# Up projections: four products of high weights, then four of low weights, for each tile of x

## The chip, the cores and the metric

The kernel runs on one core of a Trainium2 chip (trn2). The metric is device time in microseconds for one execution of the whole program. The engines that matter are TensorE (PE for its products, PEld for the loads of the weights that stand still in its array), VectorE (DVE), ScalarE (ACT) and SyncE (SP), whose queue issues the DMA loads. TensorE's products add up in eight banks of PSUM, each 512 fp32 columns wide.

## What is computed

A two-layer encoder trunk on 256 tokens of width 2048: each layer is a token mixer (layer 0 dilated and grouped-query attention, layer 1 latent attention) and a gated convolutional channel mixer. All is fp32. Cut to the part that the change touches:

```python
def conv_glu(h, w_up, conv_w, conv_b, w_down):
    u = h @ w_up                                   # (256, 2048) @ (2048, 11264)
    gate, val = u[..., :D_FF], u[..., D_FF:]       # D_FF = 5632
    gate = depthwise_conv3(gate, conv_w, conv_b)
    return (jax.nn.gelu(gate, approximate=False) * val) @ w_down

# in each layer:
h = rms_norm(x, p['ffn_pre'])
x = x + rms_norm(conv_glu(h, *p['ffn']), p['ffn_post'])
```

## The kernel before

Every fp32 product is made from parts that TensorE takes at a faster rate (the type fp32r): an operand is split into a high part, its rounding to fp32r, and a low part, the rest. A product is then high x high + high x low + low x high; low x low is dropped.

**Weights.** They come in chunks of 128 x 1024, in a fixed order over the whole program. `weights()` returns the current chunk's two parts and issues the work for the next ones: the load by SP's queue into one of four `raw` buffers (line 156), the rounding on ACT into one of three `whi` buffers (line 173), and the subtraction on DVE into one of three `wlo` buffers (line 174). As a rule the parts of two further chunks are issued ahead, so a buffer is written again as soon as the products that read it are done.

**Up projection.** `ffn` runs over 11 groups of 512 gate columns; for each it calls `proj_t` twice, for the gate columns (`pg`, banks of the tag "acc") and for the value columns (`pv`, banks "at"). So there are 22 such calls in a layer and 44 in all. A call has 8 chunks, each with the weights of two tiles of x (k = 2c and 2c + 1; x has 16 tiles of 128 features) for 512 output columns, which are four blocks of 128, one bank each. The weights stand still in the array. What streams through it is x(k): 256 columns of its high part and 256 of its low part side by side. A product with high weights (line 244) streams all 512, giving high x high in one half of the bank and high x low in the other. A product with low weights (line 245) streams the first 256 alone and adds low x high into the first half.

**After a call.** `joined` (lines 305 and 306) copies one half of a bank out on ACT and adds the other on DVE. The gate goes on through the norm's factor (986), the convolution (987 to 990) and gelu (992), the value through 997 and 998 and a split (585, 586). All this shares ACT's and DVE's queues with the splitting of the weights for the next call, which uses the other four banks.

**Around the up projections.** Before the first group, the residual is added (454), x is transposed tile by tile on TensorE (478) and split into `xhl` by ACT and DVE (590, 591); this goes on while the first group's products run. After the last group, `down` runs the down projection (1101, 1102, 1104), partly by a scheme with seven products for eight, whose sums (1005, 76) are made by DVE at its start.

**Order.** The program is written as one list, and a compile-time planner turns it into one queue per engine. It weighs priorities (the order of the program) against its own estimate of when each operand is ready, so instructions of one engine can stand in another order than written. Each queue then runs in order. Transposes and a few others are kept in the written order by `keep_in_program_order`.

Of the kernel before, what the change touches and what calls it, by code (L numbers as in the profile page):

```python
# [16 lines left out]
P = 128  # L17
T = 256
# [68 lines left out]
class Model:  # L87
# [146 lines left out]
    def proj_t(self, nk, x, tag):  # L234

        mm = self.nc.tensor.matmul
        out = [self.psum(tag) for _ in range(4)]
        for c in range(nk // 2):
            hi, lo = self.weights()
            for i in range(4):  # L240
                for kk in range(2):
                    k = 2 * c + kk
                    s = slice(kk * 512 + i * P, kk * 512 + (i + 1) * P)
                    mm(out[i], hi[:, s], x(k), start=k == 0, stop=False)  # L244
                    mm(out[i][:, :T], lo[:, s], x(k)[:, :T], start=False, stop=k == nk - 1)  # L245
            self.tick()
        return out

# [998 lines left out]
```

## Time and profile before

| what | value |
|---|---|
| time, median of 3 runs | 2061.9 us (2061.72 to 2062.07) |
| profiled execution, span from the first to the last instruction | 2060.1 us |
| TensorE products: busy, count | 2043.4 us (99%), 10905 |
| DVE busy | 1478.4 us (72%) |
| ACT busy | 1129.3 us (55%) |
| mean granted TensorE clock | 0.998 |
| products of line 244 (512 columns) | 2816 |
| products of line 245 (256 columns) | 2816 |
| up projections, start of the first to start of the last product | layer 0 from 331.1 us, layer 1 to 1817.9 us |

The profiled execution has no time listed apart from its span; the span is 1.8 us below the median of the runs. In the rows, "idle" is the time an engine stood still in front of an instruction, and what follows the arrow is what ended that idle time. A product's recorded duration runs into the next one's, since products are pipelined; the step from one product's start to the next one's is what it costs in a stream.

### The profile page before, as it was taken

The page shows a single profiled execution, that of the slowest core. Times are in us where ns is not written, and L with a number is a line of the kernel's source. Part 1 is how long each engine was busy: PE and PEld are TensorE (multiplying, and loading weights), DVE is VectorE, ACT ScalarE, POOL GpSimd, SP SyncE. Part 2 cuts the span into 40 slices and gives each one's busy share as a digit, 9 for nine tenths or more (in the row PEclk, how much of TensorE's full clock was granted, in tenths as well). Part 3 has the DMA queues.
Part 4 walks back from the last instruction along what each step waited for, and adds up shares of the span by engine and source line. Part 5 has one row for each costly group of instructions (what it writes and reads, how often), then busy time and mean ns, then how long its engine had stood idle before and what let it go on. Part 6 is the DMA issues. An engine that isn't in the chain of part 4 may idle for free.

```text
span 2060.1 us, 29196 instructions
## 1 busy us (share of the span) xinstructions
PE 2043.4 (99%) x10905; PEld 1750.0 (85%) x10905; DVE 1478.4 (72%) x2263; ACT 1129.3 (55%) x1753; POOL 0.2 (0%) x4
## 2 busy tenths in 40 slices
PE   9999999999999999999999999999999999999998
PEld 7888888888888888888878998888888888888886
DVE  6877757766766767878787875676766766787877
ACT  6655546555555555555465664555555555554553
POOL 0000000000000000000000000000000000000000
PEclk9999999999999999999999999999999999999999
DMA  8545566666566666566655445566566566556664
GB/s 318 176 153 161 166 197 193 186 194 193 185 194 191 185 194 189 184 211 197 203 179 170 124 134 173 176 210 189 185 193 193 184 195 193 185 184 205 204 206 141
DMA packets 108717, 385.96 MB, mean 187 GB/s; under 512 B 12064, under 2 KB 12576, under 8 KB 108576
## 3 DMA queue, kind: packets, MB, share of 16 engines
q1 hardware_dynamic: 108288, 383.83, 59.3%
q8 instruction: 85, 1.39, 0.3%
q14 instruction: 56, 0.46, 0.1%
q10 hardware_dynamic: 288, 0.28, 0.0%
HBM read 381.96 MB, written 2.10 MB: 186 GB/s over the span
## 4 chain that ended last, share of the span: by engine, by line
PE 96%; DVE 3%; issue 0%; ACT 0%; DMA 0%; DVEq 0%; SPq 0%; ACTq 0%
PE ps L244 31%; PE ps L245 16%; PE ps L230 8%; PE ps L231 8%; PE ps L232 8%; PE ps L1104 7%; PE ps L1101 7%; PE ps L1102 7%; PE ps L537 1%; PE ps L300 1%; DVE x L454 1%; DVE wlo L174 1%; PE ps L478 0%; DVE sums L1005 0%; DMA raw<-in_w_in 0%
## 5 line engine op out<-in xcount | busy, mean ns | idle before, releaser
L174 DVE TENSOR_TENSOR wlo<-raw,whi 128x1024 fp32r<-128x1024 f32 (+1 forms) x662 | 807.6, 1221 | 490.3 <-ACT whi L173 487.6
L173 ACT CAST whi<-raw 128x1024 fp32r<-128x1024 f32 (+1 forms) x662 | 694.3, 1050 | 642.7 <-PE ps L244 302.4
L244 PE MATMUL ps<-xhl,whi 128*128 128x512 f32 x2816 | 978.7, 394 | 1.0 <-DVE xhl L591 1.0
L245 PE MATMUL ps<-xhl,wlo 128*128 128x256 f32 x2816 | 779.2, 277 | 0.0
L244 PEld LDWEIGHTS ps<-xhl,whi 128*128 128x128 f32 x2816 | 527.6, 188 | 123.1 <-DVE xhl L591 2.0
L245 PEld LDWEIGHTS ps<-xhl,wlo 128*128 128x128 f32 x2816 | 528.9, 188 | 1.0 <-DVE wlo L174 0.5
L1101 PE MATMUL ps<-whi,gh 128*128 128x512 f32 x584 | 227.3, 389 | 0.0
L1102 PE MATMUL ps<-whi,gl 128*128 128x512 f32 x584 | 227.2, 389 | 0.0
L1104 PE MATMUL ps<-wlo,gh 128*128 128x512 f32 x584 | 182.0, 390 | 0.8 <-DVE wlo L174 0.8
L230 PE MATMUL ps<-whi,xhl 128*128 128x512 f32 x352 | 138.7, 395 | 0.9 <-ACT whi L173 0.8
L231 PE MATMUL ps<-wlo,xhl 128*128 128x512 f32 x352 | 137.6, 391 | 0.0
L232 PE MATMUL ps<-whi,xhl 128*128 128x512 f32 x352 | 137.2, 390 | 0.0
L1104 PEld LDWEIGHTS ps<-wlo,gh 128*128 128x128 f32 x584 | 109.1, 188 | 25.2 <-DVE wlo L174 2.7
L1101 PEld LDWEIGHTS ps<-whi,gh 128*128 128x128 f32 x584 | 109.6, 188 | 22.8
L1102 PEld LDWEIGHTS ps<-whi,gl 128*128 128x128 f32 x584 | 109.6, 188 | 22.8
L230 PE MATMUL ps<-whi,oh 128*128 128x512 f32 x256 | 100.0, 390 | 0.0
L231 PE MATMUL ps<-wlo,oh 128*128 128x512 f32 x256 | 99.7, 389 | 0.0
L232 PE MATMUL ps<-whi,ol 128*128 128x512 f32 x256 | 99.6, 389 | 0.0
L305 ACT COPY half<-ps 128x256 f32<-128x256 f32 x176 | 65.1, 370 | 43.9 <-PE ps L244 34.6
L230 PEld LDWEIGHTS ps<-whi,xhl 128*128 128x128 f32 x352 | 66.0, 188 | 14.5 <-ACT whi L173 1.1
L232 PEld LDWEIGHTS ps<-whi,xhl 128*128 128x128 f32 x352 | 66.1, 188 | 13.9
L231 PEld LDWEIGHTS ps<-wlo,xhl 128*128 128x128 f32 x352 | 66.3, 188 | 13.4 <-DVE wlo L174 0.9
(211 smaller groups left out, 2061.0 us busy)
## 6 DMA issues: line engine op xcount, KB each, us to landing
raw<-in_w_up SPq DMA_DIRECT2D x352, 512.0 KB, 4.1
raw<-in_w_down SPq DMA_DIRECT2D x128, 512.0 KB, 3.9
raw<-in_w_in SPq DMA_DIRECT2D x88, 512.0 KB, 3.7
raw<-in_w_out SPq DMA_DIRECT2D x64, 512.0 KB, 4.1
seven_a<-in_w_down SPq DMA_DIRECT2D x24, 512.0 KB, 4.5
seven_b<-in_w_down SPq DMA_DIRECT2D x24, 512.0 KB, 4.2
gb<-in_post SPq DMA_DIRECT2D x16, 256.0 KB, 3.8
raw<-in_w_qn SPq DMA_DIRECT2D x8, 512.0 KB, 3.6
```

Of the source, the lines that this page charges most:

```text
L173: self.nc.scalar.copy(hi[:, s], raw[:, s])
L174: self.nc.vector.tensor_tensor(out=lo[:, s], in0=raw[:, s], in1=hi[:, s].bitcast(F32), op=ALU.subtract)
L230: mm(ps, lh, rh, start=start, stop=False)
L231: mm(ps, lh, rl, start=False, stop=False)
L232: mm(ps, ll, rh, start=False, stop=stop)
L244: mm(out[i], hi[:, s], x(k), start=k == 0, stop=False)
L245: mm(out[i][:, :T], lo[:, s], x(k)[:, :T], start=False, stop=k == nk - 1)
L300: self.tc.keep_in_program_order(self.nc.tensor.transpose(out, x, self.ident))
L305: self.nc.scalar.copy(b, ps[:, T:])
L1101: mm(bank, xh, w[0][:, c], start=start, stop=False)
L1102: mm(bank, xl, w[0][:, c], start=False, stop=False)
L1104: mm(bank, xh, w[1][:, c], start=False, stop=stop)
```

## The change

In `proj_t`, the loop over the two tiles of x in a chunk becomes the outer one. For each tile, four products of high weights go to the four banks, then four products of low weights go to the same four banks. Each bank gets the same products in the same order of k; the first product of a bank still clears it, and its last product is still the low one of the last tile.

```diff
         for c in range(nk // 2):
             hi, lo = self.weights()
-            for i in range(4):
-                for kk in range(2):
-                    k = 2 * c + kk
-                    s = slice(kk * 512 + i * P, kk * 512 + (i + 1) * P)
-                    mm(out[i], hi[:, s], x(k), start=k == 0, stop=False)
-                    mm(out[i][:, :T], lo[:, s], x(k)[:, :T], start=False, stop=k == nk - 1)
+            for kk in range(2):
+                k = 2 * c + kk
+                s = [slice(kk * 512 + i * P, kk * 512 + (i + 1) * P) for i in range(4)]
+                for i in range(4):
+                    mm(out[i], hi[:, s[i]], x(k), start=k == 0, stop=False)
+                for i in range(4):
+                    mm(out[i][:, :T], lo[:, s[i]], x(k)[:, :T], start=False, stop=k == nk - 1)
             self.tick()
```

## The prediction

> **What bounds the kernel now.** I read the page first: its engines, its chain, its groups.
>
> ```profile
> span 2060.1 us, 29196 instructions
> PE 2043.4 (99%) x10905; PEld 1750.0 (85%) x10905; DVE 1478.4 (72%) x2263; ACT 1129.3 (55%) x1753; POOL 0.2 (0%) x4
> PE 96%; DVE 3%; issue 0%; ACT 0%; DMA 0%; DVEq 0%; SPq 0%; ACTq 0%
> L244 PE MATMUL ps<-xhl,whi 128*128 128x512 f32 x2816 | 978.7, 394 | 1.0 <-DVE xhl L591 1.0
> L245 PE MATMUL ps<-xhl,wlo 128*128 128x256 f32 x2816 | 779.2, 277 | 0.0
> ```
>
> TensorE (PE) is busy for 99% of the span and is 96% of the chain that ended last. L244 and L245 are the 2816 long products (512 columns, high weights) and 2816 short ones (256 columns, low weights) that the change reorders; TensorE idled 1.0 us in front of them in the whole run. Their mean durations (394 and 277 ns) overlap, since matmuls are pipelined, so they are no prices. What counts is start to start. So I went to the table by windows, for a stretch that holds one group of eight chunks, and to the timeline of TensorE, where the first and last row of a run and the count between them give the interval.
>
> ```profile
> 401.21:423.40 22.19, 22.19 (x131) 19.41 (x130) 15.45 (x25) 13.10 (x20) 0.00 (x0) 1.00 0.62 191
> ```
>
> ```profile
> 559.63 0.40 PE L244 MATMUL ps<-xhl,whi 128*128 128x512 f32 x1
> 559.87 0.28 PE L245 MATMUL ps<-xhl,wlo 128*128 128x256 f32 x1
> 559.98 0.39 PE L244 MATMUL ps<-xhl,whi 128*128 128x512 f32 x1
> ...
> 565.87 0.40 PE L244 MATMUL ps<-xhl,whi 128*128 128x512 f32 x1
> ```
>
> The first window's columns are length, then busy time of PE, PEld, DVE, ACT, POOL, then the granted clock (1.00). A group of 64 pairs takes 22.19 us, and TensorE is busy for all of it: 346.7 ns a pair. The timeline agrees: 18 pairs between 559.63 and 565.87, 6.24 us, 346.7 ns a pair. All 2816 pairs are then 976 us, 47% of the span. Nothing but TensorE's own rate sets this time, so the first question is what that rate becomes in the new order.
>
> **The change part by part: the products.** No product is added or removed: each chunk keeps 8 long and 8 short ones, with as many weight loads. Only the neighbours change. Eight products were long, short, long, short, ...; now they are four long, then four short. Of the eight intervals, one long-to-short and one short-to-long stay (together 346.7 ns); three long-to-short and three short-to-long become three long-to-long and three short-to-short. Both new kinds stand elsewhere in this trace: long after long in the output projection (first fence), short after short in layer 1's attention (second).
>
> ```profile
> 259.68 0.39 PE L230 MATMUL ps<-whi,oh 128*128 128x512 f32 x1
> 259.90 0.39 PE L231 MATMUL ps<-wlo,oh 128*128 128x512 f32 x1
> ...
> 303.88 0.39 PE L230 MATMUL ps<-whi,oh 128*128 128x512 f32 x1
> ```
>
> ```profile
> 1142.27 0.28 PE L232 MATMUL ps<-ckv,wlo 128*128 128x256 f32 x1
> 1142.39 0.28 PE L230 MATMUL ps<-cq,whi 128*128 128x256 f32 x1
> ...
> 1145.15 0.28 PE L232 MATMUL ps<-cq,wlo 128*128 128x256 f32 x1
> 1145.27 0.28 PE L230 MATMUL ps<-pT,v 128*128 128x256 f32 x1
> ```
>
> Long to long: 195 intervals in 44.20 us, 226.67 ns. Short to short: 24 intervals from 1142.39 to 1145.27, 2.88 us, 120.0 ns. Together 346.67 ns, what a long-short pair takes now. Two points on a line also give what is paid per product whatever its length: 2 x 120.0 - 226.67 = 13.3 ns, and the pair in alternation pays it twice, no more. So the three swapped pairs cost 3 x (346.67 - 346.7) = 0 in each of the 704 sets of eight (2816 / 4). Bounds: rows are rounded to 0.01 us, so the short interval is known to about 0.4 ns, the long one to 0.05 ns and the pair by the window to 0.2 ns; I allow 0.5 ns, over 2112 swapped pairs +-1.1 us. I take 0.
>
> In the new order every product goes to another bank than the one before it, where now four in a row accumulate into one. The short run above crosses from one psum tile to the next at 1142.27 to 1142.39 and at 1145.15 to 1145.27, and both steps are 0.12 us like the rest; I price the rotation at nothing, inside the same bound.
>
> **The first group of a layer.** There x is still being made when the projection starts.
>
> ```profile
> PE ps L244 <- DVE xhl L591: 1.0, 2, 0.5
> PE ps L1104 <- DVE wlo L174: 0.8, 2, 0.4
> ```
>
> ```profile
> 331.07 0.49 PE L244 MATMUL ps<-xhl,whi 128*128 128x512 f32 x1
> ...
> 331.75 0.28 PE L245 MATMUL ps<-xhl,wlo 128*128 128x256 f32 x1
> 332.51 0.50 PE L244 MATMUL ps<-xhl,whi 128*128 128x512 f32 x1 [0.48 <-DVE xhl L591]
> ```
>
> ```profile
> 331.59 0.87 DVE L591 SCALAR_TENSOR_TENSOR xhl<-ps,gains,xhl 128x256 fp32r<-128x256 f32 x2
> ```
>
> The chain of waits has two waits of 0.5 us on xhl, one per layer. The old order wants the second tile of x after one pair of the first bank; the new one finishes all four banks with the first tile, 4 x 0.347 = 1.39 us of work, first. The two L591 end at 332.46, and the projection's first product started at 331.07, so work for the first tile lasts till 332.46 and the wait goes. I take the whole 0.5 us twice: -1.0 us. Bounds: 0 (the planner orders these products otherwise) and -1.5 us (the 0.76 us step from 331.75 to 332.51 less a normal 0.12 is 0.64 us, and a little more around it, twice). What is late next is the low half of the second chunk's weights, which the new order wants 3 x 0.227 = 0.68 us later than the old.
>
> **Buffers and queues.** The high weights of a chunk are read for the last time four short products before a chunk's end instead of one, 3 x 0.120 = 0.36 us earlier, so the cast that waits for that buffer on ACT, the subtraction on DVE behind it, and the load on SP's queue that waits for the raw buffer come 0.36 us earlier in steady state. None of them is on the path (TensorE idles 0.0 us for weights there), so this is worth nothing, and its cover is the 22.19 us of a group in which DVE works 15.45 and ACT 13.10. The queues' contents stay the same; the planner that orders them may shift some.
>
> The other end is worse off. A bank's sum is finished later: bank 0's last product was the 4th of the last chunk's 16 and becomes the 13th. It used to be done 2 x 0.347 = 0.69 us into the chunk and is now done at 4 x 0.347 + 4 x 0.227 + 0.12 = 2.41 us: 1.72 us later. Bank 1 is 1.15 us later, bank 2 0.57, bank 3 the same. What is behind it on ACT and DVE at a group's end:
>
> ```profile
> 709.05 0.39 PE L244 MATMUL ps<-xhl,whi 128*128 128x512 f32 x1
> ```
>
> ```profile
> 709.13 1.05 ACT L173 CAST whi<-raw 128x1024 fp32r<-128x1024 f32 x1 [1.72 <-PE ps L244]
> 710.08 0.37 ACT L305 COPY half<-ps 128x256 f32<-128x256 f32 x1
> 710.63 0.37 ACT L305 COPY half<-ps 128x256 f32<-128x256 f32 x1 [0.18 <-PE ps L245]
> ```
>
> ```profile
> 711.36 0.75 DVE L306 TENSOR_TENSOR g<-ps,half 128x256 f32<-128x256 f32 x2
> 712.02 0.75 DVE L986 TENSOR_TENSOR g<-g,rb 128x256 f32<-128x256 f32 x2
> 713.22 1.23 DVE L174 TENSOR_TENSOR wlo<-raw,whi 128x1024 fp32r<-128x1024 f32 x1 [0.45 <-ACT whi L173]
> 717.28 1.22 DVE L174 TENSOR_TENSOR wlo<-raw,whi 128x1024 fp32r<-128x1024 f32 x1
> ```
>
> The last chunk starts at 709.05. Copies move from 710.08 and 710.63 to about 711.80 and 712.17, and the first addition (L306) from 711.36 to about 712.17: 0.8 us later, of which the idle 0.45 us before 713.22 takes up more than half. Who waits: the subtraction that ends at 718.50 makes the low weights of the chunk that starts at 709.05 + 4 x 2.773 = 720.14 (eight pairs of 346.7 ns are 2.773 us; three buffers rotate). Now they are wanted at 720.14 + 0.23, with 1.87 us to spare; in the new order at 720.14 + 0.91, so 2.55 us less the delay of some 0.4 to 0.8. No wait comes of it, at any of the 42 group ends inside the two layers: 0. Without that cover each microsecond of excess would cost 42 us.
>
> At the last group's end the cover is missing, because the down projection's sums fill DVE:
>
> ```profile
> 822.75:841.40 18.65, 18.28 (x81) 14.59 (x80) 18.64 (x32) 10.65 (x15) 0.00 (x0) 1.00 0.38 115
> ```
>
> ```profile
> 822.29 0.77 DVE L306 TENSOR_TENSOR u<-ps,half 128x256 f32<-128x256 f32 x2
> ...
> 839.46 1.21 DVE L174 TENSOR_TENSOR wlo<-raw,whi 128x1024 fp32r<-128x1024 f32 x1
> ```
>
> ```profile
> 819.98 0.39 PE L244 MATMUL ps<-xhl,whi 128*128 128x512 f32 x1
> ...
> 840.73 1.20 PE L1104 MATMUL ps<-wlo,gh 128*128 128x512 f32 x4 [0.37 <-DVE wlo L174]
> ```
>
> DVE is busy for 18.64 of these 18.65 us, and at the end TensorE waits for the subtraction that ends at 840.67. The first addition stands at 822.29; the last chunk starts at 819.98, so bank 0 is done at 819.98 + 2.41 = 822.39, its copy ends near 822.97, and the addition starts 0.7 us later. With no idle time to take it up, TensorE's wait grows by as much: +0.7 us a layer, +1.4 us. Bounds: 0 (the planner puts other DVE work in the hole) and +2 us.
>
> **The sum.** 0 + (-1.0) + 0 + 1.4 = +0.4 us: the profiled execution's span of 2060.1 becomes 2060.5. The three runs without a profile have a median of 2061.9, 1.8 us above that span for what lies around it, so I predict 2062.3. About 0.2% (4.1 us) is what a measurement can tell from no change, so this is no change.
>
> **The rivals.** *Late evacuation (slower).* If the planner puts a cast (1.05 us) ahead of the first copy at each group's end and all of bank 0's 1.72 us passes through, the third chunk's low weights come 2.77 us later, 0.22 us more than the 2.55 us there are: 42 x 0.22 = 9.2 us, 2071. It decides from 2.55 us of delay; 0.10 us beyond that passes the 4.1 us. For it: all four banks now finish within 0.36 us. Against it: the 0.45 us of idle DVE time, and that banks 2 and 3 were evacuated long after they were ready anyway. 5%.
>
> *Short products in a row are bound by their weight loads (slower).*
>
> ```profile
> 1142.40 0.19 PEld L231 LDWEIGHTS ps<-cq,whi 128*128 128x128 f32 x1
> ```
>
> A load is recorded at 0.19 us, longer than the 120 ns between short products. If loads ran ahead, alternation would even them out (two loads per 346.7 ns) and four shorts in a row would not: at worst (0.19 - 0.12) x 2112 = +148 us, 2210, and 2 ns each already passes 0.2%. Against it stand the 24 intervals of 120.0 ns with such a load before each. [...] That loads overlap products the trace agrees with (loads of 0.19 us at steps of 0.12). 2%.
>
> *Rotating banks (faster).* If the 13.3 ns paid per product were the turn-round in one bank, rotation would save up to 5632 x 13.3 = 75 us, 1987. The two tile crossings at 0.12 us speak against it; together with unseen stalls, 4%.
>
> *Rotating banks (slower clock).* If rotation made TensorE pause, its clock could drop; the windows show 1.00 throughout.
>
> ```profile
> L214 PE MATMUL ps<-zeros x63: 272/273/421, 1.1 to 1325.3; 128*128 128x256 bf16 x63
> ```
>
> The slowest warm-up product took 421 against 273 ns, 1.54 times; a tenth of the up projections at that pace is 0.1 x 976 x 0.54 = 53 us, 2115. [...] In this trace the crossings above leave no gap. 1%.
>
> *The change doesn't do what it says.* The planner may issue the products in an order of its own; the time is then 2061.9, inside the forecast.
>
> **How the numbers follow.** No change has 88%. Faster: 4% for the banks and 2% for the small terms all falling one way, 6%. Slower: 5 + 2 + 1 = 8%, less the 2% of late evacuation that stays under 4.1 us, 6%. The forecast's own terms reach from 2061.9 - 1.1 - 1.5 = 2059.3 to 2061.9 + 1.1 + 2.0 = 2065.0. That is 88% by itself; half a microsecond more at each end covers the spread of the runs (0.35 us): 2058.8 to 2065.5.
>
> **What would show it.** Right: a window over a group of eight chunks still reads 22.19 us; long to long 227 ns and short to short 120 ns; the wait on xhl gone from the first group; the wait on wlo at the start of the down projection up by about 0.7 us per layer; no new wait on wlo at L245. Wrong: a group that takes 22.28 us or more (4.1 us over 44 groups is 0.09 us each), or a wait on wlo in the third chunk of each group, or a granted clock under 1.00.

## The result

The changed kernel takes 2074.9 us (median of 6, 2074.8 to 2075.4), against 2062.0 for the kernel before beside it: 12.9 us or 0.6% slower between medians. Over all runs of both the ratio is 1.0051, interval 1.0032 to 1.0069. The ratio is lower than the medians say because two of the six executions of the kernel before took 2071 us; the experiments show why, and times below are compared with its quick executions, near 2062. The profiled execution of the changed kernel spans 2073.1 us, 13.0 more than that of before. The forecast was 2062.3, no change, with a range from 2058.8 to 2065.5.

From here on a group is one call of `proj_t`, eight chunks, as in the prediction: 22 groups a layer. The windows table of the first layer, first of the kernel before, then of the changed one, is cut at the same events: first group of a layer, the other 21 groups, the first 200 products of the down projection. Columns: window, length, busy time of PE, PEld, DVE, ACT, POOL, clock, DMA share, GB/s.

```profile
331.07:356.75 25.68, 25.20 (x151) 21.71 (x149) 21.41 (x37) 19.94 (x42) 0.00 (x0) 1.00 0.66 216
356.75:822.75 466.00, 466.00 (x2691) 407.55 (x2690) 321.48 (x510) 254.08 (x381) 0.00 (x0) 1.00 0.62 190
822.75:868.99 46.24, 45.87 (x202) 37.35 (x201) 42.09 (x59) 25.01 (x30) 0.00 (x0) 1.00 0.58 182
```

```profile
331.08:356.56 25.48, 24.99 (x150) 21.92 (x149) 20.74 (x35) 18.87 (x39) 0.00 (x0) 1.00 0.68 217
356.56:828.26 471.70, 471.70 (x2692) 412.05 (x2691) 321.88 (x510) 250.63 (x382) 0.00 (x0) 1.00 0.62 188
828.26:875.55 47.29, 45.99 (x202) 37.35 (x201) 42.46 (x60) 26.46 (x33) 0.00 (x0) 1.00 0.57 177
```

Of the 13.0 us, the second line brings 5.7 us in each layer, 11.4 in all (layer 1, cut the same way, is 5.69 longer). TensorE is busy for the whole window in both kernels, at a clock of 1.00: it waits for nobody, its products just come more slowly. The third line brings 1.05 us here and 1.03 in layer 1. The first gives back 0.2 and 0.3.

The slower stream, in the timeline of TensorE (start, length, line, count):

```profile
499.88 1.09 PE L244 MATMUL ps<-xhl,whi 128*128 128x512 f32 x4
500.81 0.64 PE L246 MATMUL ps<-xhl,wlo 128*128 128x256 f32 x4
501.28 1.09 PE L244 MATMUL ps<-xhl,whi 128*128 128x512 f32 x4
502.21 0.63 PE L246 MATMUL ps<-xhl,wlo 128*128 128x256 f32 x4
502.68 0.40 PE L244 MATMUL ps<-xhl,whi 128*128 128x512 f32 x1
```

Eight products take 1.40 us (499.88 to 501.28 to 502.68) where 4 x 0.3467 = 1.387 were predicted. Four longs take 0.93 us, 232 ns each and not 227; four shorts 0.47, 118 ns and not 120. By the starts in the trace a chunk is 2806.7 ns against 2773.3 before, in every chunk behind the first groups except the one right behind each of them (some 2.98 us against 2.86). The 334 others make 33.3 ns x 334 = 11.1 us, and those two 0.2 us: together nearly all of the 11.4.

### The profile page after: what moved, and what is told of

Read it like the earlier page. It is cut to its first block, busy times and chain, and to the rows that moved or that the text cites. A ratio compares the mean times of both kernels' runs of the same rounds, so it can differ in the third digit from the quotient of the medians.

```text
span 2073.1 us, 29158 instructions
## 1 busy us (share of the span) xinstructions
PE 2054.0 (99%) x10905; PEld 1759.2 (85%) x10905; DVE 1478.4 (71%) x2263; ACT 1122.8 (54%) x1753; POOL 0.2 (0%) x4
## 4 chain that ended last, share of the span: by engine, by line
PE 96%; DVE 2%; ACT 1%; issue 0%; DMA 0%; DVEq 0%; SPq 0%; ACTq 0%
PE ps L244 32%; PE ps L246 16%; PE ps L232 8%; PE ps L231 8%; PE ps L230 8%; PE ps L1105 7%; PE ps L1102 7%; PE ps L1103 7%; PE ps L538 1%; PE ps L301 1%; DVE x L455 1%; DVE wlo L174 1%; PE ps L479 0%; ACT whi L173 0%; DVE sums L1006 0%
## 5 line engine op out<-in xcount | busy, mean ns | idle before, releaser
L244 PE MATMUL ps<-xhl,whi 128*128 128x512 f32 x2816 | 771.8, 395 | 1.0 <-DVE xhl L592 1.0
L244 PEld LDWEIGHTS ps<-xhl,whi 128*128 128x128 f32 x2816 | 481.1, 189 | 66.4 <-DVE xhl L592 1.4
L246 PEld LDWEIGHTS ps<-xhl,wlo 128*128 128x128 f32 x2816 | 432.9, 189 | 59.8
L246 PE MATMUL ps<-xhl,wlo 128*128 128x256 f32 x2816 | 450.4, 281 | 0.0
L1105 PE MATMUL ps<-wlo,gh 128*128 128x512 f32 x584 | 182.0, 390 | 0.8 <-DVE wlo L174 0.8
L1105 PEld LDWEIGHTS ps<-wlo,gh 128*128 128x128 f32 x584 | 109.1, 188 | 25.2 <-DVE wlo L174 2.7
L306 ACT COPY half<-ps 128x256 f32<-128x256 f32 x176 | 60.5, 369 | 48.2 <-DVE g L307 25.1
```

Of the source, the lines that this page charges most:

```text
L244: mm(out[i], hi[:, s[i]], x(k), start=k == 0, stop=False)
L246: mm(out[i][:, :T], lo[:, s[i]], x(k)[:, :T], start=False, stop=k == nk - 1)
L306: self.nc.scalar.copy(b, ps[:, T:])
L1105: mm(bank, xh, w[1][:, c], start=False, stop=stop)
```

## The experiments

The theories at the start. *Grouping*: a long product right after a long one is what costs. *Rotation*: a product that goes to another bank, or the same x streamed eight times, is what costs. The numbers below "a chunk" are from the starts of products in the trace of each run, over the groups behind the first.

**Pairs rotated.** Long and short alternate, but the tile of x is the outer loop:

```diff
+            for kk in range(2):
+                k = 2 * c + kk
+                for i in range(4):
+                    mm(out[i], hi[:, s], x(k), ...)
+                    mm(out[i][:, :T], lo[:, s], x(k)[:, :T], ...)
```

> Tile of x outermost as in the changed kernel, but each bank gets its long product and then its short one before the next bank: the lengths alternate as before, the bank changes after every second product, and x(k) is read by eight products in a row. Grouping theory (a long product right after a long one is what costs): alternation is kept, so a chunk takes 2.773 us and the run about 2062. Rotation theory (going to another bank, or reading x(k) eight times in a row, is what costs): half of the changes of bank of the changed kernel stay, a chunk takes 2.79 us or more and the run about 2068.

Measured: 2061.8 us (median of 10), but not one time: six executions at 2061.5 to 2061.9, three at 2070.5 to 2070.7, one at 2079.4. The profiled one was a 2070.6, and shows both rates in one execution. Two windows of 200 us, one in each layer:

```profile
401.00:601.00 200.00, 200.00 (x1134) 173.41 (x1134) 136.10 (x215) 108.38 (x163) 0.00 (x0) 1.00 0.61 186
1401.00:1601.00 200.00, 200.00 (x1155) 174.92 (x1154) 137.94 (x217) 109.86 (x164) 0.00 (x0) 1.00 0.63 190
```

Layer 0 gets through 1134 products, layer 1 through 1155, with TensorE never idle and the same clock: 353.3 and 346.7 ns a pair by the starts, each kept to the layer's end. (The slow rate is a cycle of three pairs that takes 1060 ns where three quick pairs take 1040, so 353.3 is a mean.) Alternation has two rates 6.7 ns a pair apart, 9 us over one layer, which is the step between the executions. Neither theory had that. The quick layer rotates banks and costs nothing, so rotation alone is not the price.

**Two and two**, bank outermost as before:

```diff
+            for i in range(4):
+                for kk in range(2):
+                    mm(out[i], hi[:, s[kk]], x(2 * c + kk), ...)
+                for kk in range(2):
+                    mm(out[i][:, :T], lo[:, s[kk]], x(2 * c + kk)[:, :T], ...)
```

> Bank outermost as before; for each bank the two long products of the chunk's two tiles, then the two short ones: long, long, short, short into one bank. Grouping theory: 4 long-long steps a chunk where the changed kernel has 6, so two thirds of its 33 ns: about 2.795 us a chunk, run about 2070. Rotation theory: no more changes of bank than before, 2.773 us a chunk, about 2062.

Measured: 2067.4 us (2067.1 to 2067.5, n = 10), 5.3 above the quick executions beside it; over all executions the ratio is 1.0019 (1.0007 to 1.0031). A chunk takes 2786.7 ns, 13.3 more than alternation at its quick rate:

```profile
500.15 0.63 PE L244 MATMUL ps<-xhl,whi 128*128 128x512 f32 x2
...
502.94 0.63 PE L244 MATMUL ps<-xhl,whi 128*128 128x512 f32 x2
```

It costs without any new change of bank, but less than grouping by long-long steps said (22 ns).

**All products long**, in the old order and in the new:

```diff
-                    mm(out[i][:, :T], lo[:, s], x(k)[:, :T], ...)
+                    mm(out[i], lo[:, s], x(k), ...)
```

> Order of the kernel before, but the products of low weights stream all 512 columns too (which adds low x low, an extra term). All 16 products of a chunk are long, four in a row into one bank. Rotation theory: 226.7 ns a product as in the output projection, 3.63 us a chunk. Grouping theory: every step is long after long, about 233.5 ns, 3.74 us a chunk.

> Order of the changed kernel, with the products of low weights at 512 columns too (low x low added). All 16 products of a chunk are long, each to another bank. Both theories: about 233.5 ns a product, 3.74 us a chunk. If it is 226.7 ns and 3.63 us, then neither long after long nor the rotation costs anything, and the cost lies in the mix of lengths alone.

Measured: 2360.4 and 2360.3 us, one execution each. The timeline of the second (new order):

```profile
500.36 1.07 PE L246 MATMUL ps<-xhl,wlo 128*128 128x512 f32 x4
...
543.88 1.07 PE L246 MATMUL ps<-xhl,wlo 128*128 128x512 f32 x4
```

24 sets of eight longs in 43.52 us: 226.7 ns a product, and 3626.7 ns a chunk in both kernels. Both theories fall. Long after long, with these weights, this x and rotating banks, is as quick as in the output projection (226.7 ns in both). What costs is that lengths are mixed. New theory, *length*: the sequence of lengths alone sets the extra time. Rival, *bank*: in a mixed stream rotation still matters.

**Eight and eight** (both tiles' high weights, then both tiles' low ones):

> Order of the changed kernel, but with both tiles' products of high weights first: eight long, then eight short, banks rotating. A chunk without extra time is 2773.3 ns, the changed kernel's 2806.7 (33.3 more). If the extra time is paid at each change of length: 2 changes a chunk where the changed kernel has 4, so 2790 ns, run about 2069. If it is paid by each long product that follows a long one in a mixed stream (7 such steps a chunk instead of 6): 2812 ns or more, run about 2077.

Measured: 2070.2 us (2070.1 to 2070.3, n = 8), 2793.3 ns a chunk, 20.0 more than quick alternation.

```profile
499.64 2.00 PE L244 MATMUL ps<-xhl,whi 128*128 128x512 f32 x8
501.48 1.11 PE L248 MATMUL ps<-xhl,wlo 128*128 128x256 f32 x8
502.43 2.00 PE L244 MATMUL ps<-xhl,whi 128*128 128x512 f32 x8
504.27 1.11 PE L248 MATMUL ps<-xhl,wlo 128*128 128x256 f32 x8
505.23 1.09 PE L244 MATMUL ps<-xhl,whi 128*128 128x512 f32 x4
```

Eight longs take 1.84 us, 27 ns over 8 x 226.7; eight shorts 0.95 to 0.96, a little under 0.96. Step by step, the eight longs take 233, 236, 228, 232, 231, 227, 227, 227 ns and the shorts 113, 119, then 120 six times. After a run of shorts some five longs are slow, then the rate is that of the unmixed stream. So the extra is paid after a turn from short to long (27 ns on the longs, of which the shorts give back 7: 20 ns in all when the runs are long enough), and not on each long-long step, which would have made 2812 ns. Fewer turns with longer runs cost less than four and four (33 ns a chunk).

**Two and two, rotated** (the same lengths, other banks):

> Two long products for banks 0 and 1, their two short ones, then the same for banks 2 and 3: the sequence of lengths of the two-and-two experiment (long, long, short, short), which took 2786.7 ns a chunk within one bank, but now with a change of bank at every product and one x(k) for all eight. Length theory (the sequence of lengths alone decides): 2786.7 ns again, run about 2067. Bank theory (rotation costs where lengths mix): nearer to the changed kernel, 2800 ns or more, run about 2072.

Measured: 2066.2 us (2065.8 to 2066.3, n = 8), 2786.7 ns a chunk, the same as within one bank:

```profile
501.75 0.63 PE L245 MATMUL ps<-xhl,whi 128*128 128x512 f32 x2
...
504.53 0.40 PE L245 MATMUL ps<-xhl,whi 128*128 128x512 f32 x1
```

**All products short:**

```diff
-                    mm(out[i], hi[:, s[i]], x(k), ...)
+                    mm(out[i][:, :T], hi[:, s[i]], x(k)[:, :T], ...)
...
+                    mm(out[i][:, T:], hi[:, s[i]], x(k)[:, T:], ...)
```

> Order of the changed kernel, with each long product cut into two short ones (256 columns of the high part of x, then 256 of the low part): 24 short products a chunk, all of one length, banks rotating. Length theory: an unmixed stream has no extra time, 24 x 120.0 = 2880 ns a chunk. Bank theory, or a cost of many short products in a row in this stage: more than 2880, by 2.8 ns a product or more (2950).

Measured: 2098.0 us (one execution).

```profile
499.72 0.64 PE L246 MATMUL ps<-xhl,whi 128*128 128x256 f32 x4
...
523.72 0.52 PE L244 MATMUL ps<-xhl,whi 128*128 128x256 f32 x3
```

50 rows of four between the two starts: 200 products in 24.00 us, 120.0 ns each. Unmixed shorts have no extra either, banks rotating.

**One bank:**

```diff
+                b = out[k % 4]
                 for i in range(4):
-                    mm(out[i], hi[:, s[i]], x(k), ...)
+                    mm(b, hi[:, s[i]], x(k), ...)
```

> The changed kernel's sequence of products with the same weights and the same x, but all eight products of one tile of x go to one bank, so that sums of different columns are added together (the output leaves the right sums out). Length theory: 2806.7 ns a chunk, as the changed kernel. Bank theory: 2773.3 ns.

Measured: 2070.2 us (one execution) and 2806.7 ns a chunk, with the changed kernel's pattern of steps: 1.40 us for eight products.

```profile
500.64 1.09 PE L245 MATMUL ps<-xhl,whi 128*128 128x512 f32 x4
501.56 0.64 PE L247 MATMUL ps<-xhl,wlo 128*128 128x256 f32 x4
502.04 1.09 PE L245 MATMUL ps<-xhl,whi 128*128 128x512 f32 x4
```

The length theory holds in all four runs: banks play no part in the rate (two and two 2786.7 ns a chunk within one bank and rotated, four and four 2806.7 rotated and into one bank). (The run is 4.7 us quicker than the changed kernel, outside the groups: by the starts 1.7 to 1.8 us at each down projection and 0.6 in each first group. Two of its banks are finished a chunk earlier, which would explain the former.)

Two questions were left: what picks the rate of alternation, and what the 2.1 us at the down projections are. In the next two runs, two longs and two shorts are put into the alternation to see whether they set its rate anew ("relock").

**Relock in each chunk, and once a call.** Alternation in the old order, with the last four products of a chunk going long, long, short, short:

```diff
+            pairs = [p for i in range(6) for p in (hs[i], ls[i])]   # once a call: range(8 if c else 6)
+            if len(pairs) < 16:
+                pairs += [hs[6], hs[7], ls[6], ls[7]]
```

> Order of the kernel before (long, short alternating, bank outermost), except that the last four products of each chunk go long, long, short, short. Alternation has been seen at two rates, 346.7 and 353.3 ns a pair. If the rate hangs on what the stream did just before (a phase), two longs and two shorts in each chunk set it anew each time, and all executions take the same time: about 2063 us if they set the quick rate (6 x 346.7 + 696.7 = 2776.7 ns a chunk), about 2077 if the slow one. If the rate is set from outside (by the chip, or once at a layer's start), executions scatter: near 2063, 2070 and 2077.

> The same with long, long, short, short only at the end of the first chunk of each of the 44 calls, all else alternating. Phase theory: one time in all executions, the one that the relock in each chunk gives, about 2062 (or 2079 if the slow rate is set). Outside theory: scatter as in the kernel before, 2062, 2071 and 2080.

Measured in each chunk: 2069.9 us (2069.6 to 2070.3, n = 10); ratio 1.0023 (1.0007 to 1.0038). No scatter, so the phase theory holds, but in a way it had not named. First products of four chunks in a row:

```profile
421.35 0.40 PE L253 MATMUL ps<-xhl,whi 128*128 128x512 f32 x1
...
424.17 0.40 PE L253 MATMUL ps<-xhl,whi 128*128 128x512 f32 x1
...
426.94 0.40 PE L253 MATMUL ps<-xhl,whi 128*128 128x512 f32 x1
...
429.76 0.40 PE L253 MATMUL ps<-xhl,whi 128*128 128x512 f32 x1
```

2.82, 2.77, 2.82 us: here two longs and two shorts turn the slow rate into the quick one and the quick one into the slow one, chunk after chunk. Once a call: 2080.0 us (2079.9 to 2080.2, n = 4), ratio 1.0072 (1.0046 to 1.0098); all executions take the time of two slow layers. One whole call of the trace:

```profile
379.57:402.18 22.61, 22.61 (x131) 19.60 (x129) 14.89 (x25) 10.86 (x17) 0.00 (x0) 1.00 0.60 186
```

At the quick rate it would take 22.19 us, at the slow one 22.61. By the starts all 42 calls behind the first groups are slow, so here the same four products switched nothing. They are no plain switch, then. By the starts they fall on another place of the slow rate's cycle of three pairs: on its first pair in the run that switches, on its third in the run that does not. That this decides was not tested.

**Last chunk old:** the changed kernel, with the last chunk of each call in the old order.

```diff
+            old = c == nk // 2 - 1
+            if old:
+                todo = [(low, i, kk) for i in range(4) for kk in range(2) for low in range(2)]
+            else:
+                todo = [(low, i, kk) for kk in range(2) for low in range(2) for i in range(4)]
```

> The changed kernel, but the last chunk of each call keeps the old order, so that banks 0 to 2 end as early as before. Seven of eight chunks at 2806.7 ns and one at 2773.3 take about 1.4 us off the changed kernel's 2074.9. If the 2.1 us that the changed kernel loses at the start of the two down projections come from the late banks, they go too: 2071.4. If they have another cause (the planner's order, weights): 2073.5.

Measured: 2071.6 us (2071.4 to 2071.8, n = 8), where late banks gave 2071.4. The waits of TensorE, of the changed kernel and of this one:

```profile
PE ps L1102 <- ACT whi L173: 1.8, 2, 0.9
PE ps L1105 <- DVE wlo L174: 0.8, 2, 0.4
```

```profile
PE ps L251 <- DVE xhl L597: 1.0, 2, 0.5
PE ps L1110 <- DVE wlo L174: 0.9, 2, 0.5
```

The down projection's wait on the high weights, 0.9 us in each layer, goes when the banks end early, and the first 200 products of the down projection take what they took before (46.24 us):

```profile
827.72:873.88 46.16, 45.70 (x203) 37.45 (x202) 41.95 (x59) 25.93 (x31) 0.00 (x0) 1.00 0.56 183
```

(The line numbers move with the edit: L1105 and L1110 are one product, and L251 is L244.)

**First chunk new**, all else old: `old = c > 0` in the same edit.

> The reverse of the last-chunk experiment: the first chunk of each call goes in the changed kernel's order (four long, four short, twice), the other seven in the order of the kernel before. In the last-chunk experiment the old-order chunk that followed groups of four took the quick rate (276 + 140 ticks a pair, 346.7 ns). Phase theory: the group of four at each call's start sets the quick rate for the seven chunks behind it, in every execution: 44 x 33 ns over the kernel before at its best, 2063.5 us, with no executions near 2071 or 2080. Outside theory: scatter in steps of about 8 us.

Measured: 2063.9 us (2063.4 to 2064.4, n = 11), and no execution elsewhere; the kernel before, on the same chip, 2062.1 in eleven executions and 2070.8 to 2071.1 in four. Ratio 0.9999 (0.9987 to 1.0012). The windows of one call's first chunk and of the next seven:

```profile
512.67:515.47 2.80, 2.80 (x19) 2.45 (x17) 2.80 (x7) 2.48 (x6) 0.00 (x0) 1.00 0.60 193
515.47:534.86 19.39, 19.39 (x114) 17.09 (x113) 12.06 (x19) 8.39 (x11) 0.00 (x0) 1.00 0.63 190
```

Seven chunks of 2.773 would be 19.41; the window ends 0.03 us before the next call, and by the starts the seven take 19.42. So the chunks behind the groups of four products are quick, with one exception. In layer 1 the call right behind the first group stays slow to its end, and the call after it is quick again:

```profile
1352.93:1375.70 22.77, 22.77 (x132) 19.62 (x130) 15.65 (x25) 13.91 (x21) 0.00 (x0) 1.00 0.59 184
1375.70:1397.91 22.21, 22.21 (x131) 19.57 (x130) 14.83 (x25) 10.85 (x16) 0.00 (x0) 1.00 0.64 190
```

The last-chunk run has the same exception at the same call. So by the starts the groups of four gave the quick rate in 41 of the 42 calls behind the first groups, and the one miss was mended a call later; that may be why these executions spread over 0.9 us. (A tick in the expectation is a unit of mine, 346.67 / 416 = 0.833 ns: the 226.67 ns of a long in an unmixed stream are 272, the 120.0 of a short 144.)

## Why the prediction was wrong

**Products (predicted 0, measured +11.4 us): the step that failed.** It was "the three swapped pairs cost 3 x (346.67 - 346.7) = 0". Both prices in it are right and were met again (226.7 in all-long, 120.0 in all-short), but they come from streams of one length. The line through them, 13.3 ns a product whatever the neighbour, holds in such streams alone. That alternation takes exactly 226.67 + 120.0 made it look general. It is no proof: alternation also runs at 353.3 (pairs rotated, layer 0), two and two at 348.3, four and four at 350.8, eight and eight at 349.2 ns a pair. What the runs showed in place of 0 is 16.7 ns for each of the 704 sets of eight. The warning stood in the rows quoted: 559.63, 559.87, 559.98 put the long's step at 0.24 and the short's at 0.11, not at 0.227 and 0.120. Only their sum fitted, which was luck, and I used the sum.

The price could also have been read in the trace of the kernel before. Its attention stages turn from shorts to longs and back, for instance in layer 0:

```profile
80.01 0.88 PE L537 MATMUL ps<-kB,q 128*128 128x256 f32 x6
80.73 0.40 PE L230 MATMUL ps<-whi,xhl 128*128 128x512 f32 x1
...
81.66 0.39 PE L231 MATMUL ps<-wlo,xhl 128*128 128x512 f32 x1
```

The four longs behind the shorts take 0.93 us (80.73 to 81.66), where 4 x 226.7 is 0.907. By the starts, all 25 such turns of that trace with at least eight longs behind them cost about 27 ns on the longs, some 23 of it on the first four; where at least eight shorts follow longs, the shorts give 7 to 8 ns back in 17 of 18 places. Four and four then cost 15 to 16 ns a set, and 704 sets 11 us: an estimate from the trace of before that comes out near the 11.4 measured. The prediction took its prices from runs of one length and left out the turns.

**Rotation of banks: right at nothing.** All long rotated (226.7 ns a product), two and two rotated (2786.7 ns a chunk, as within one bank), and one bank (2806.7, as the changed kernel) show it directly.

**Short products bound by their loads: not seen.** That loads run ahead far enough to even out, as this rival has it, no run shows: by the starts, a load at the up projections begins 1 to 5 ns after the product in front of its own in 5597 of 5632 cases in the kernel before and in 5602 in the changed one, and later in the rest. So it is one product ahead at most, in both orders. Shorts in a row took 120.0 ns in all short.

**Slower clock by rotation: not seen.** The clock is 1.00 in every window above. TensorE was busy for all of the 471.70 us; the 0.48 us that it idled in the first group of the kernel before left the clock at 1.00 too. In the trace of before it falls once, after the last product:

```profile
2050.00:2051.00 1.00, 0.61 (x3) 0.18 (x1) 1.00 (x3) 0.00 (x0) 0.00 (x0) 1.00 0.00 0
...
2053.00:2054.00 1.00, 0.00 (x0) 0.00 (x0) 0.93 (x4) 0.00 (x0) 0.00 (x0) 0.60 0.93 361
2054.00:2055.00 1.00, 0.00 (x0) 0.00 (x0) 0.96 (x3) 0.00 (x0) 0.00 (x0) 0.50 0.43 164
```

TensorE has no work from 2050.61 on, and the clock reads 1.00 until 2053, 0.60 in the next microsecond and 0.50 behind it. No such stretch stands in the up projections.

**First group (predicted -1.0, measured -0.5 us), and not by the step named.** The wait on xhl stayed:

```profile
331.65 0.39 PE L246 MATMUL ps<-xhl,wlo 128*128 128x256 f32 x2
332.53 0.73 PE L244 MATMUL ps<-xhl,whi 128*128 128x512 f32 x2 [0.49 <-DVE xhl L592]
```

The planner starts with two long and two short products, not with four and four. In the kernel before, too, two pairs ran ahead of the wait (331.07 to 331.75), not the one pair that the prediction named. So the work ran out as early as before. The 0.2 and 0.3 us were gained elsewhere in the group: TensorE's idle time in layer 0 is the same (0.48 and 0.49 us by the windows), and what gave the gain is not shown.

**The 42 group ends: right at nothing.** No wait of TensorE on weights at L244 or L246 is left in the changed kernel's list, and the chunk's length does not change across a group's end.

**Start of the down projections (predicted +1.4, measured +2.1 us): the sign was right, two steps were not.** I moved the first addition by 0.7 us in the old queue order, and let all of the delay through to TensorE. But the planner made another order: ACT works a sum of the down projection first, DVE stands idle for it, and the addition comes 1.83 us after the last chunk's end (830.09 against 828.26) where it had come 0.46 before it.

```profile
828.95 1.23 DVE L587 TENSOR_TENSOR seven<-sums,seven 128x1024 fp32r<-128x1024 f32 x1 [1.12 <-ACT seven L586]
830.09 0.75 DVE L307 TENSOR_TENSOR u<-ps,half 128x256 f32<-128x256 f32 x2
```

Then TensorE waits, now for the high weights too:

```profile
846.15 0.50 PE L1102 MATMUL ps<-whi,seven 128*128 128x512 f32 x1 [0.91 <-ACT whi L173]
846.49 0.39 PE L1103 MATMUL ps<-whi,seven 128*128 128x512 f32 x1
847.27 1.19 PE L1105 MATMUL ps<-wlo,gh 128*128 128x512 f32 x4 [0.39 <-DVE wlo L174]
```

That the late banks cause this is shown by the last-chunk experiment. But the delay did not pass through one for one. With pairs rotated, bank 0 also ends later, and the addition starts 0.63 us after the last chunk's end (831.66), 1.1 us later than before; the same 200 products then take no longer than the 46.24 us of before:

```profile
832.29 0.75 DVE L306 TENSOR_TENSOR u<-ps,half 128x256 f32<-128x256 f32 x2
```

```profile
831.66:877.84 46.18, 45.80 (x203) 37.37 (x202) 42.06 (x60) 25.28 (x30) 0.00 (x0) 1.00 0.57 182
```

In layer 0, two and two rotated delays it by 1.2 us and loses nothing (46.20), eight and eight by 1.9 and loses 0.7, the changed kernel by 2.3 and loses 1.05. So about 1.2 us of delay were free in these runs, and by this the 0.7 that I had worked out would have cost nothing; that the forecast came near the measured 2.1 is luck. What covers the 1.2 us is not shown.

## What to carry to other kernels

The price of a product in TensorE's stream was not a property of the product here: four longs took 232 ns each in the changed kernel and 226.7 in an unmixed stream. Price a new order from a stream with the same sequence of lengths. Where none is there, look in the trace for turns from one length to the other, read the single steps behind a turn and not the middle of a run, and take their spread times their number as the bound. Of the orders tried here, alternation at its quick rate was the cheapest (346.7 ns a pair) and four and four the dearest of the grouped ones (350.8); but alternation also has a slow rate that cost more than any of them (353.3). When a stage is bound by such a stream, look at several executions, since one order had two rates here.

## What the hardware showed

Unmixed streams of these fp32r products run at 226.7 ns (512 columns, both runs of all long) and 120.0 ns (256, all short), within 0.01 us of an even pace over 126 to 200 products. That is 0.44 and 0.47 ns a column; the fp32 transposes of line 300 (128 columns) follow each other at 109 ns in the trace of before, 0.85 a column. Mixed streams took extra time that depends on the sequence, per long and short: alternating 0 or 6.7 ns, two and two 1.7, four and four 4.2, eight and eight 2.5. Left alone, alternation kept whichever of its two rates it had to the end of the layer (both layers of pairs rotated and of the kernel before). Two longs and two shorts switched it in one run, each time, and never in another. Groups of four gave the quick rate in 41 of 42 calls of a trace, and 11 of 11 executions near 2064. Otherwise the rate differs from execution to execution of one kernel; that the irregular first group of a layer decides it is likely, but not shown. Of the 74 executions of the kernel before on record, 47 took about 2062, 26 about 2071 and one 2079.7, while the changed kernel took 2074.8 to 2075.4 in all six, so the change is a loss against all but that one. No version tried is quicker than 2061.5 to 2062.3, which alternation reaches at its quick rate; first chunk new holds 2063.9 without the slow executions.

The extra time of a chunk came out as 0, 13.3, 20.0, 33.3 and, at the slow rate, 53.3 ns on average: all multiples of 6.7 ns. What in TensorE makes a turn of length cost time, and why in these steps, stays open: the trace shows starts of products and of loads, not what a load waits for. Whether the time is lost in the weight loads was not tried, since no product here goes without one (10905 of each in the kernel before). The trace of the kernel before has one hint: in layer 1, from 1107.90 us on, long and short products alternate whose weights have 64 columns instead of 128, and by the starts they settle at 227 and 113 ns, 340 a pair where the quick rate is 346.7. Their output is smaller as well, so this is no test.
